# Layer 1's query projection moved ahead of the head loop, and three elementwise steps of the heads moved to GpSimd

## The chip, the core and the metric

The kernel runs on one core of one Trainium2 chip. The metric is device time in microseconds, the median of several executions; a profile is one further execution, recorded by the hardware profiler. PE is TensorE (matmuls and transposes), DVE is VectorE, ACT is ScalarE, POOL is GpSimd, SP is the engine that issues most DMAs.

## The reference

Two layers work on 1024 latent tokens of width 1024 and 256 context tokens. Layer 0 (attention heads beside mLSTM heads) is the same before and after. Layer 1 has 16 bidirectional gated-linear-attention heads with 128 keys and 128 values each; only the latent stream is returned. What it computes:

```python
def project(h):                                    # h: (1, T, 1024), w_in: (1024, 5 * 2048)
    q, f_fwd, f_bwd, i, z = _split_cols(h @ w_in, C_SIZES)       # each 2048 = 16 heads x 128
    def decay(f_pre):
        f = lb + (1.0 - lb) * jax.nn.sigmoid(f_pre)
        return 1.0 - f, jnp.log(f)                 # k and the log decay
    return (silu(q), i, (decay(f_fwd), decay(f_bwd))), z
...
def step(S, xs):                                   # per head, both directions, chunk by chunk
    qc, kc, vc, lfc = xs
    b = jnp.cumsum(lfc, axis=2)
    o = einsum('bhtk,bhkv->bhtv', qc * jnp.exp(b), S)
    pair = jnp.exp(where(tri, b[:, :, :, None, :] - b[:, :, None, :, :], -inf))
    a = einsum('bhtk,bhtsk->bhts', qc, pair * kc[:, :, None, :, :])
    o = o + einsum('bhts,bhsv->bhtv', a, vc)
    bL = b[:, :, -1:, :]
    S = jnp.exp(bL[:, :, 0])[..., None] * S + einsum('bhsk,bhsv->bhkv', kc * jnp.exp(bL - b), vc)
...
return (_rms(o, h_norm) * silu(z)) @ w_out         # added to x with a gate
```

## The kernel before

**Products in two parts.** An fp32 operand is split into a high part (a cast on ACT, line 74) and a low part (the difference, on DVE, line 75, function `split`). A dense product is three matmuls per 128 rows of the contraction: high by high, high by low, low by high (`dense`, lines 127 to 129). In the profile they are the matmuls `mm<-hh,wh`, `mm<-hl,wh`, `mm<-hh,wl`; `hh` and `hl` are the two parts of the normalised input, which stay in SBUF, transposed.

**The stage ahead of the heads** (pool `qv`) computes v and z of layer 1 for all heads, 512 columns at a time. It treats the product as a 2 by 2 product of quarters and forms it with seven products in place of eight (`q_seven`: sums of input quarters `s1` to `s4` made once, sums of weight quarters made per group by `q_form`). For z each of the seven products is two units of 12 matmuls with 512 moving columns (`tr=True`); a unit's result goes to PSUM, is combined on DVE, passed through silu (`z_sink`: sigmoid on ACT, multiplication on DVE) and stored to DRAM by a POOL DMA, as `zd[head]`. The groups run in the order v0 v1 z0 v2 z1 v3 z2 z3 (v0 by the plain eight products).

**The heads.** `build` loops over 16 heads. Three things of neighbouring heads are issued in each turn:

- `hg_intra` of head h: for each half of 512 tokens (first half 1, then half 0) K = 1 - F, two products Q = q x F, then seven levels (`hg_level`). A level copies a selection of K (`gksel`, ACT, line 1226; at level 0 also one of Q, line 1230), multiplies it with Q on PE (line 1235, four 128x128 products), takes the result over into `gA` under a mask (DVE; at level 6 two copies on ACT, lines 1245 and 1246), and multiplies K and Q by decays on DVE (line 1256). After level 0, `hg_diag` uses the sum of the two K directions, made on DVE (line 1243). At the end K is transposed on PE (line 1210) into PSUM tiles of tag `tr` and copied to `gkn`, one direction by ACT, the other by DVE (line 1212). `gK` has two buffers, one for each half, so a half's next K cannot be written before these transposes have read the last one.
- `hg_scan` of head h-1: 15 state products (`s<-gv,gkn`, line 1281) with a DVE step each, and three output products per chunk (`acc`, lines 1297 to 1299); four ACT squares and a POOL reciprocal root per four chunks (lines 1305, 152, 154).
- `hg_parts` of head h+1: the projections f of both directions (512, 512 and 256 tokens each) and q (512 and 512), each with 24 matmuls per token block, and `hg_ctx`. The weights come as 128 columns in two pieces of 256 KB, each split by line 74 and line 75. They wait in a ring of four slabs, that is two blocks of weights.

PSUM has eight banks: tag `mm` two (projections), `tr` two (transposes), `s` three, `acc` one. A tile scheduler orders each engine's instructions by priority and readiness in its own model; on the chip every engine then runs its list strictly in that order.

Of the kernel before, what the change touches and what calls it, by code (L numbers as in the profile page):

```python
# [9 lines left out]
F32 = mybir.dt.float32  # L10
F32R = mybir.dt.float32r
U8 = mybir.dt.uint8
AF = mybir.ActivationFunctionType
# [5 lines left out]
P = 128  # L19
# [27 lines left out]
class Prog:  # L47
# [24 lines left out]
    def split(self, hi, lo, x):  # L72
        nc = self.nc
        nc.scalar.copy(hi, x)  # L74
        nc.vector.tensor_tensor(out=lo, in0=x, in1=hi.bitcast(F32), op=ALU.subtract)  # L75
# [747 lines left out]
    def hg_parts(self, h, pool, w=None):  # L823
# [20 lines left out]
        def q(t0):  # L844
            ps = self.ps("mm", [P, 512])
            self.proj_tr(ps, weights(0), 0, t0, 512)
            t = st["q"][t0 // 512] = self.t(pool, [P, 512], F32, "gq", 2)
            nc.scalar.activation(t, ps, AF.Sigmoid)
            nc.vector.tensor_tensor(out=t, in0=t, in1=ps, op=ALU.mult)
# [158 lines left out]
    def z_sink(self, j, pool):  # L1008
        def sink(c, t, m, o):
            g = self.t(pool, [P, 512], F32, "qg", 2)  # L1010
            self.nc.scalar.activation(g, o, AF.Sigmoid)
            self.nc.vector.tensor_tensor(out=o, in0=g, in1=o, op=ALU.mult)
            s = t // self.half * 512
            self.nc.gpsimd.dma_start(out=self.zd[4 * j + 2 * c + t % self.half // 2, :, s : s + 512], in_=o)

        return sink
# [161 lines left out]
    def hg_intra(self, st, pool, slots):  # L1178
# [8 lines left out]
        for hf in (1, 0):  # L1187
            F, q = st["F"][hf], st["q"][hf]
            K = self.t(pool, [P, 2, n], F32, "gK", 2)
            nc.vector.tensor_scalar(out=K, in0=F, scalar1=-1.0, scalar2=1.0, op0=ALU.mult, op1=ALU.add)  # L1190
            Q = self.t(pool, [P, 2, n], F32, "gQ", 4)
            for d in range(2):
                nc.vector.tensor_tensor(out=Q[:, 1 - d, :], in0=q, in1=F[:, d, :], op=ALU.mult)
            A = self.t(pool, [P, 4, P], F32, "gA", 4)
            hv[hf] = dict(Q=Q, A=A, T=F, K=K)
# [8 lines left out]
        for hf in (1, 0):  # L1204
            H = hv[hf]
            H["kn"] = []
            for d in range(2):
                p = self.ps("tr", [P, 4, P])
                for c in range(4):
                    nc.tensor.transpose(p[:, c, :], H["K"][:, d, c * P : (c + 1) * P], self.ident)  # L1210
                k_ = self.t(pool, [P, 4, P], F32, "gkn", 4)
                (nc.vector.tensor_copy if d else nc.scalar.copy)(k_, p)
                H["kn"].append(k_)
# [3 lines left out]
    def hg_level(self, H, lev, pool):  # L1217
# [21 lines left out]
        if lev == 0:  # L1239
# [3 lines left out]
            nc.vector.tensor_tensor(out=H["ks"], in0=K[:, 0, :], in1=K[:, 1, :], op=ALU.add)  # L1243
# [26 lines left out]
    def hg_scan(self, st, halves, pool):  # L1270
# [60 lines left out]
    def build(self):  # L1331
        self.six = None
        tc, nc, a = self.tc, self.nc, self.a
        dma = nc.sync.dma_start
        with ExitStack() as es:
# [12 lines left out]
            self.zd = self.scratch(dr, "zd", [16, P, LAT])  # L1348
            self.md_all = self.scratch(dr, "md", [20, T, 256])
# [208 lines left out]
            with l1:  # L1558
                with tc.tile_pool(name="qv", bufs=1) as pool, self.pp.phase(sa=4):
                    self.q_open([(0, 2), (2, 2)], a["wc"], (pool, "qo", 3), (pool, "b11", 4), (pool, "sr", 2))  # L1560
                    cs = lambda z, j: [(3 + z) * 2048 + j * 512 + c * 256 for c in range(2)]
                    raw = self.q_raw(pool, cs(0, 0), ("12", "22"))
                    self.q_plain(raw, early, self.v_sink(0), pool)
                    self.q_sums(pool, "2", S)
                    for x in ("v1", "z0", "v2", "z1", "v3", "z2", "z3"):
                        z, j = x[0] == "z", int(x[1])
                        self.q_seven(self.q_raw(pool, cs(z, j)), S, self.z_sink(j, pool) if z else self.v_sink(j), pool, tr=z)
# [11 lines left out]
                scan, done = [], [None, None]  # L1579
                for h in range(16):  # L1580
# [12 lines left out]
                    done, st = [done[1], st], nxt  # L1593
                self.hg_y(14, done[0], pool, self.yd2)
# [178 lines left out]
```

## Time and profile before

| | us |
|---|---|
| time, median of 3 runs (3436.0 to 3436.93) | 3436.47 |
| the profiled execution's own time | 3440.12 |
| its span in the profile | 3438.4 |
| PE busy | 3398.6 (99%) |
| DVE busy | 2347.2 (68%) |
| ACT busy | 1498.9 (44%) |
| POOL busy | 502.9 (15%) |

The stage ahead of the heads lies at about 1850 to 2160 us of the span, the heads at about 2160 to 3290 us. An engine's busy time is the union of its instructions; matmuls are pipelined, so two that follow each other overlap in the record and the distance of their starts says more than their duration. An fp32 product of 128x128 is recorded as two matmuls ("x8" for four products). In a row of the timeline the columns are start, duration, engine, line, operation, result and operands, shapes and count; the bracket gives the idle time before it and what ended that.

### The profile page before, as it was taken

To read this page: it belongs to the slowest core of one execution; us is meant where nothing else is said; L and a number is where in the kernel's file an instruction comes from. 1 tells how busy PE (TensorE), PEld (TensorE's weight loads), DVE (VectorE), ACT (ScalarE), POOL (GpSimd) and SP (SyncE) were. 2 spreads that over 40 slices of the span, in tenths; PEclk is the share of its full clock that TensorE was granted. 3 is DMA by queue.
4 is the path that set the end of the run, shared out by engine and by line. 5 is a ranking of instruction groups with operands and counts; after the bars stand their busy time and mean duration, and the time that the engine had idled before them with its cause. 6 is when DMAs were issued, how large, how long until landed. Compare 5 with 4: busy or idle time off the path is not lost. (4 is left out here: it accounts for less than half of the span.)

```text
span 3438.4 us, 62336 instructions
## 1 busy us (share of the span) xinstructions
PE 3398.6 (99%) x23360; PEld 3060.1 (89%) x23360; DVE 2347.2 (68%) x5814; ACT 1498.9 (44%) x3469; POOL 502.9 (15%) x834
## 2 busy tenths in 40 slices
PE   7999999999999999999999999999999999999999
PEld 5689999999999999988879998899999999999887
DVE  5477747666666654667678666577777777777855
ACT  5322245555544534556546323444444444444431
POOL 3111121222222211212212111000000000000010
PEclk9999999999999999999999999999999999999999
DMA  8543322332223235465483332211111111111345
GB/s 264 190 134 110 120 69 57 88 88 78 80 77 88 77 91 160 139 181 162 141 255 128 109 106 91 77 41 61 54 50 53 60 54 50 53 60 55 114 140 179
DMA packets 359518, 359.63 MB, mean 105 GB/s; under 512 B 30584, under 2 KB 304184, under 8 KB 359088
## 3 DMA queue, kind: packets, MB, share of 16 engines
q1 hardware_dynamic: 315248, 246.36, 24.3%
q0 software_dynamic: 43824, 109.16, 9.2%
q8 instruction: 184, 3.01, 0.4%
q14 instruction: 118, 0.97, 0.1%
q10 hardware_dynamic: 144, 0.13, 0.0%
HBM read 271.98 MB, written 83.42 MB: 103 GB/s over the span
## 5 line engine op out<-in xcount | busy, mean ns | idle before, releaser
L129 PE MATMUL mm<-hh,wl 128*128 128x512 f32 (+1 forms) x1564 | 567.8, 363 | 1.8 <-DVE wl L75 1.8
L127 PE MATMUL mm<-hh,wh 128*128 128x512 f32 (+1 forms) x1564 | 565.0, 361 | 0.1
L128 PE MATMUL mm<-hl,wh 128*128 128x512 f32 (+1 forms) x1564 | 564.6, 361 | 0.0
L127 PE MATMUL mm<-wh,hh 128*128 128x256 f32 x1880 | 541.6, 289 | 2.5 <-ACT wh L74 2.4
L128 PE MATMUL mm<-wl,hh 128*128 128x256 f32 x1880 | 542.1, 289 | 0.1
L129 PE MATMUL mm<-wh,hl 128*128 128x256 f32 x1880 | 541.9, 289 | 0.2 <-DVE hl L75 0.2
L127 PEld LDWEIGHTS mm<-wh,hh 128*128 128x128 f32 x1880 | 358.0, 191 | 5.1 <-ACT wh L74 2.6
L128 PEld LDWEIGHTS mm<-wl,hh 128*128 128x128 f32 x1880 | 358.7, 191 | 3.7 <-issue 1.7
L129 PEld LDWEIGHTS mm<-wh,hl 128*128 128x128 f32 x1880 | 358.4, 191 | 3.4 <-issue 1.6
L127 PEld LDWEIGHTS mm<-hh,wh 128*128 128x128 f32 x1564 | 296.3, 189 | 42.5 <-issue 4.2
L128 PEld LDWEIGHTS mm<-hl,wh 128*128 128x128 f32 x1564 | 296.1, 189 | 41.0 <-issue 4.2
L129 PEld LDWEIGHTS mm<-hh,wl 128*128 128x128 f32 x1564 | 295.8, 189 | 40.8 <-DVE wl L75 2.0
L74 ACT CAST wh<-wraw 128x512 fp32r<-128x512 f32 x292 | 179.8, 621 | 267.3 <-PE mm L128 157.9
L1226 ACT COPY gksel<-gK 128x512 f32<-128x512 f32 x224 | 148.3, 663 | 274.6 <-PE s L1235 262.8
L75 DVE TENSOR_TENSOR wl<-wraw,wh 128x512 fp32r<-128x512 f32 x292 | 197.0, 684 | 58.6 <-ACT wh L74 56.4
L1235 PE MATMUL s<-gQ,gksel 128*128 128x128 f32 x1536 | 202.1, 276 | 0.0
L1235 PEld LDWEIGHTS s<-gQ,gksel 128*128 128x128 f32 x1536 | 192.6, 191 | 5.8
L776 PE MATMUL mm<-woh,yh 128*128 128x512 f32 (+1 forms) x420 | 167.6, 399 | 2.4 <-ACT yh L74 2.4
L778 PE MATMUL mm<-woh,yl 128*128 128x512 f32 (+1 forms) x420 | 167.1, 399 | 0.5 <-DVE yl L75 0.4
L777 PE MATMUL mm<-wol,yh 128*128 128x512 f32 (+1 forms) x420 | 165.1, 394 | 0.0
L1256 DVE TENSOR_TENSOR gQ<-gQ,gT 128x256 f32<-128x256 f32 x384 | 143.1, 413 | 21.2 <-PE s L1235 21.2
L1248 DVE COPY_PREDICATED gA<-glm,s 128x512 f32<-128x512 uint8 x160 | 117.2, 733 | 54.5 <-PE s L1235 54.5
(592 smaller groups left out, 7971.5 us busy)
## 6 DMA issues: line engine op xcount, KB each, us to landing
wraw<-in_wc_dram SPq DMA_DIRECT2D x130, 256.0 KB, 3.0
wraw<-yd SPq DMA_DIRECT2D x116, 256.0 KB, 4.2
wraw<-in_wab_dram SPq DMA_DIRECT2D x98, 256.0 KB, 3.3
md<-ev POOLq DMA_DIRECT2D x78, 256.0 KB, 2.8
adar<-in_wada_dram POOLq DMA_DIRECT2D x16, 1024.0 KB, 5.9
b<-in_wc_dram SPq DMA_DIRECT2D x62, 256.0 KB, 3.1
adar<-in_wada_dram SPq DMA_DIRECT2D x16, 512.0 KB, 11.1
wraw<-in_wab_dram SPq DMA_DIRECT2D x64, 128.0 KB, 2.7
```

Of the source, the lines that this page charges most:

```text
L74: nc.scalar.copy(hi, x)
L75: nc.vector.tensor_tensor(out=lo, in0=x, in1=hi.bitcast(F32), op=ALU.subtract)
L127: mm(ps, lhsT=lh(k), rhs=rh(k), start=(first and k == 0), stop=False)
L128: mm(ps, lhsT=lh(k), rhs=rl(k), start=False, stop=False)
L129: mm(ps, lhsT=ll(k), rhs=rh(k), start=False, stop=(last and k == nk - 1))
L776: mm(ps, lhsT=yh[:, k, :], rhs=w.h(k)[:, cols], start=(k == 0), stop=False)
L777: mm(ps, lhsT=yh[:, k, :], rhs=w.l(k)[:, cols], start=False, stop=False)
L778: mm(ps, lhsT=yl[:, k, :], rhs=w.h(k)[:, cols], start=False, stop=(k == 7))
L1226: nc.scalar.copy(ksel.rearrange("p (b s i) -> p b s i", s=2, i=h), pick(K))
L1235: nc.tensor.matmul(pa[:, c, :].rearrange("p (b s i) -> p b s i", s=2, i=h), lhsT=ksel[:, c * P : (c + 1) * P], rhs=qp[:, c * nbc : (c + 1) ...
L1248: nc.vector.copy_predicated(A, self.lmask[:, lev - 1, :].unsqueeze(1).to_broadcast([P, 4, P]), pa)
L1256: nc.vector.tensor_tensor(out=t[:, i, :, s, :], in0=t[:, i, :, s, :], in1=bc(tot), op=ALU.mult)
```

## The change

q of layer 1 is no longer computed head by head. It becomes four further groups of `q_seven` in the stage ahead, in the order v0 v1 z0 q0 v2 z1 q1 v3 q2 z2 q3 z3, is passed through the same silu, and stored to a new DRAM tensor `qd`; a head loads its two halves of q by two SP DMAs of 256 KB.

Inside the loop over heads (not in the projections of head 0 ahead of it) the low parts of weights are made on POOL; K = 1 - F and the sum of the K directions move from DVE to POOL. All four `gkn` copies of a head are now on ACT. The state product of chunk 7 takes its PSUM tile from tag `tr` in place of `s`.

```diff
     def split(self, hi, lo, x):
         nc.scalar.copy(hi, x)
-        nc.vector.tensor_tensor(out=lo, in0=x, in1=hi.bitcast(F32), op=ALU.subtract)
+        (self.lo or nc.vector).tensor_tensor(out=lo, in0=x, in1=hi.bitcast(F32), op=ALU.subtract)
...
         def q(t0):
-            ps = self.ps("mm", [P, 512])
-            self.proj_tr(ps, weights(0), 0, t0, 512)
             t = st["q"][t0 // 512] = self.t(pool, [P, 512], F32, "gq", 2)
-            nc.scalar.activation(t, ps, AF.Sigmoid)
-            nc.vector.tensor_tensor(out=t, in0=t, in1=ps, op=ALU.mult)
+            nc.sync.dma_start(out=t, in_=self.qd[h, :, t0 : t0 + 512])
...
-            nc.vector.tensor_scalar(out=K, in0=F, scalar1=-1.0, scalar2=1.0, op0=ALU.mult, op1=ALU.add)
+            nc.gpsimd.tensor_scalar(out=K, in0=F, scalar1=-1.0, scalar2=1.0, op0=ALU.mult, op1=ALU.add)
...
-                (nc.vector.tensor_copy if d else nc.scalar.copy)(k_, p)
+                nc.scalar.copy(k_, p)
...
-            nc.vector.tensor_tensor(out=H["ks"], in0=K[:, 0, :], in1=K[:, 1, :], op=ALU.add)
+            nc.gpsimd.tensor_tensor(out=H["ks"], in0=K[:, 0, :], in1=K[:, 1, :], op=ALU.add)
...
-            u = self.ps("s", [P, P])
+            u = self.ps("s" if c < 7 else "tr", [P, P])
...
-                    for x in ("v1", "z0", "v2", "z1", "v3", "z2", "z3"):
+                    for x in ("v1", "z0", "q0", "v2", "z1", "q1", "v3", "q2", "z2", "q3", "z3"):
...
+                self.lo = nc.gpsimd
                 for h in range(16):
```

The change also gives the scheduler another order. Two places matter below, both at the border between two heads.

PE, before: from the last transposes of a head's K (half 0) on. In the names, `tr` is a PSUM tile of transposes, `gK` the head's K, `s<-gv,gkn` a state product of the scan, `gvT` the context values, and `mm` with a 128x512 shape a projection for the next head.

```order
L1210 MATMUL tr_31281<-ident_75,gK_30594 128x128 x4
L1281 MATMUL s_31301<-gv_31017,gkn_31272 128x128
L1152 MATMUL tr_31408<-ident_75,gvT_31406 128x128 x2
L129 MATMUL mm_31473<-hh_22231,wl_31474 128x512
L127 MATMUL mm_31473<-hh_22231,wh_31475 128x512
L1281 MATMUL s_31305<-gv_31017,gkn_31272 128x128
L128 MATMUL mm_31473<-hl_22232,wh_31475 128x512
```

Twenty-four 128x512 projections and several small products stand between these transposes and the next head's first level product (`s<-gksel,gksel`, line 1235), at every border from the second to the fourteenth. PE, after, at every second border (six of them), from the products of level 6 (`s<-gQ,gksel`, line 1232) on:

```order
L1232 MATMUL s_32006<-gQ_31421,gksel_32004 128x128 x2
L1296 MATMUL acc_31872<-gS_6349_31974,gQ_30141 128x128
L1232 MATMUL s_32006<-gQ_31421,gksel_32004 128x128 x2
L1207 MATMUL tr_32035<-ident_76,gK_31419 128x128 x4
L1207 MATMUL tr_32042<-ident_76,gK_31419 128x128 x4
L1278 MATMUL s_32066<-gv_31842,gkn_32033 128x128
L1278 MATMUL s_32070<-gv_31842,gkn_32033 128x128
L1232 MATMUL s_32078<-gksel_32076,gksel_32074 128x128 x4
L1278 MATMUL tr_32062<-gv_31842,gkn_32033 128x128
L1149 MATMUL tr_32169<-ident_76,gvT_32167 128x128 x2
L1232 MATMUL s_32096<-gksel_32094,gksel_32092 128x128 x4
L1162 MATMUL tr_32180<-ident_76,gEc_32174 128x128 x4
```

Both halves' first level products now stand there without a projection between them and the transposes; at the other borders 13 projections of 512 columns and 23 of 256 remain between.

ACT, before, at the same border: copies of transposed K (`gkn`), selections of the new K and Q (`gksel`), level 6 results (`gA`), squares (`gon`), then the projection's evacuation (`gF<-mm`).

```order
L1212 COPY gkn_33382<-tr_33377 128x512
L1226 COPY gksel_33416<-gK_33392 128x512
L1245 COPY gA_32696<-s_33307 64x4x64
L1246 COPY gA_32696<-s_33307 64x4x64
L1230 COPY gksel_33418<-gQ_33394 128x512
L1305 ACTIVATE gon_32690,gss_33257<-acc_33150 128x128 x4
L1245 COPY gA_32702<-s_33322 64x4x64
L1246 COPY gA_32702<-s_33322 64x4x64
L1154 COPY gvc_33514<-tr_33511 128x256
L840 ACTIVATE gF_33575<-mm_33576 128x512
```

ACT, after, at the border of the PE rows above, in the change's own line numbers:

```order
L1223 COPY gksel_32074<-gK_32050 128x512
L1242 COPY gA_31418<-s_31991 64x4x64
L1243 COPY gA_31418<-s_31991 64x4x64
L1227 COPY gksel_32076<-gQ_32052 128x512
L1302 ACTIVATE gon_31412,gss_31979<-acc_31872 128x128 x4
L1242 COPY gA_31424<-s_32006 64x4x64
L1243 COPY gA_31424<-s_32006 64x4x64
L1209 COPY gkn_32040<-tr_32035 128x512
L1209 COPY gkn_32047<-tr_32042 128x512
L1223 COPY gksel_32092<-gK_32056 128x512
L1227 COPY gksel_32094<-gQ_32058 128x512
L840 ACTIVATE gF_32233<-mm_32234 128x512
```

The two copies that DVE made have joined the row, and the next head's second selection and the evacuation of a projection stand behind them.

More of the change, by code (lines that the diff above doesn't have):

```diff
@@ L1013, in sink @@
             s = t // self.half * 512
[L1014 removed]
+            self.nc.gpsimd.dma_start(out=dst[4 * j + 2 * c + t % self.half // 2, :, s : s + 512], in_=o)
         return sink
@@ L1331, in build @@
     def build(self):
-        self.six = None
+        self.six = self.lo = None
         tc, nc, a = self.tc, self.nc, self.a
```

13 lines of the change are left out of this document (8 added, 5 removed).

## The prediction

> **What bounds the kernel now.** I read the page first, then the busy times by stage, then one head's period: its waits and its timeline on each engine.
>
> ```profile
> PE 3398.6 (99%) x23360; PEld 3060.1 (89%) x23360; DVE 2347.2 (68%) x5814; ACT 1498.9 (44%) x3469; POOL 502.9 (15%) x834
> 2160.00:3213.00 1053.00, 1053.00 (x6935) 955.58 (x6934) 788.58 (x1935) 448.03 (x939) 55.53 (x80) 1.00 0.18 55
> 1850.00:2160.00 310.00, 310.00 (x1955) 280.60 (x1954) 214.26 (x336) 104.40 (x180) 43.37 (x72) 1.00 0.31 108
> 2377.39:2446.18 68.79, 68.79 (x460) 62.58 (x459) 52.40 (x130) 29.24 (x64) 4.15 (x7) 1.00 0.18 55
> ```
>
> After the stretch and its length, a row of the second kind gives the busy time of PE, PE's weight loads, DVE, ACT and POOL, then granted clock, DMA share and GB/s. Two stages matter: the heads (2160 to 3213) and the stage ahead of them (1850 to 2160). In both PE is busy all the time, at full clock. The last row is one period of the head loop, from one head's first reciprocal root to the next's. DVE works for 52.40 of its 68.79 us, ACT for 29.24, POOL for 4.15. The waits in this period bear it out: the longest are those of ACT and DVE for PE's products, and no row of that view has PE waiting.
>
> ```profile
> ACT gksel L1226 <- PE s L1235: 17.6, 10, 4.9
> DVE gA L1248 <- PE s L1235: 2.9, 3, 1.4
> ```
>
> So whatever takes work from PE in either stage shortens the kernel by as much, as long as PE's ordered list finds its operands ready. The whole question is whether it still does.
>
> **The change part by part.**
>
> *The products.* The heads lose 16 x 2 x 24 = 768 matmuls of 512 columns. The stage ahead gains 4 groups x 7 products x 2 units x 12 = 672 of the same shape: 96 fewer. The price of one is the distance of starts:
>
> ```profile
> 2395.00 0.40 PE L127 MATMUL mm<-hh,wh 128*128 128x512 f32 x1
> 2398.42 0.40 PE L127 MATMUL mm<-hh,wh 128*128 128x512 f32 x1
> 2100.00:2150.00 50.00, 50.00 (x219) 40.76 (x218) 37.40 (x59) 19.02 (x32) 5.96 (x11) 1.00 0.21 77
> ```
>
> The first two rows, in the heads, are 15 matmuls apart: 3.42 / 15 = 0.228 us. The third is a stretch inside groups z2 and z3: 50 / 219 = 0.228 us. Hence 175 us go, 153 come, and PE's work falls by 96 x 0.228 = **21.9 us**. The new groups run at PE's pace like the z groups: DVE works there for 37.40 of 50 us and ACT for 19.02, with everything that a group needs (weight sums, low parts, silu) in it.
>
> *The transfers.* Each is priced by its counterpart: storing q by the stores of z, loading q by the loads of z.
>
> ```profile
> zd<-qo POOLq DMA_DIRECT2D x16, 256.0 KB, 2.5
> gz<-zd SPq DMA_DIRECT2D x32, 256.0 KB, 2.7
> ```
>
> 32 stores join POOL's queue in the stage ahead, 32 more loads of weights SP's. In the heads 32 loads of q take the place of 32 weight pieces of the same 256 KB, so SP's queue has as many entries as before. q is issued six and seven slots of a turn ahead, some 40 us before it is needed, and DMA is busy for 0.18 of the period. I cost this at nothing; without that cover it would be 2.7 us per load.
>
> *DVE and ACT in the heads.* The rows of what leaves DVE, from 12 periods:
>
> ```profile
> L75 DVE TENSOR_TENSOR wl<-wraw,wh 128x512 fp32r<-128x512 f32 x98 | 65.7, 680 | 0.0
> L849 DVE TENSOR_TENSOR gq<-gq,mm 128x512 f32<-128x512 f32 x26 | 17.7, 682 | 13.8 <-ACT gq L848 13.8
> L1243 DVE TENSOR_TENSOR gksel<-gK 128x512 f32<-128x512 f32 x24 | 16.4, 681 | 0.0
> L1212 DVE COPY gkn<-tr 128x512 f32<-128x512 f32 x24 | 16.3, 680 | 0.0
> L1190 DVE TENSOR_SCALAR gK<-gF 128x1024 f32<-128x1024 f32 x24 | 16.3, 679 | 0.0
> ```
>
> Per head 8 + 2 + 2 + 2 + 2 = 16 instructions of 0.68 us leave: 10.9 us, so 41.5 remain. The period without q's 48 matmuls is 68.8 - 10.9 = 57.9 us, so DVE's share falls a little, from 76 to 72%. None of this is on the path by itself. ACT loses two casts and two sigmoids and gains two copies, about 0.6 us each: 28 of 58 us.
>
> *POOL.* It gains eight two-operand instructions of 512 columns and two one-operand ones of 1024 per head. No row shows such lengths. The nearest:
>
> ```profile
> L152 POOL TENSOR_SCALAR ar<-ar 128x8 f32<-128x8 f32 x40 | 9.1, 228 | 213.2 <-DVE ar L590 144.0 <-DVE anm L678 68.7
> L152 POOL TENSOR_SCALAR mr<-mss 128x1 f32<-128x1 f32 x40 | 8.8, 220 | 76.4 <-ACT mlo L559 76.0
> masks.py:197 POOL MEMSET ident<- 128x128 f32 x1 | 0.2, 205 | 0.3 <-POOLq L1761 0.3
> L1761 POOL MEMSET const-float32-1.0<- 128x1 f32 x1 | 0.1, 100 | 0.0
> ```
>
> A fill costs (205 - 100) / 127 = 0.8 ns per column, arithmetic on one operand (228 - 220) / 7 = 1.1. From below, 512 columns take 0.5 us and 1024 0.9; from above, with two operands read in turn, 0.22 + 512 x 2.3 ns = 1.4 us, and 0.22 + 1024 x 1.1 ns = 1.4 us for K. I take the arithmetic rows, 1.4 us: 14 us more per head, POOL at 18 of 58 us. [...]
>
> Who waits for POOL? The low parts: weights wait in a ring of two blocks, and between the end of one block and the first use of the one that replaces it lie the 24 short matmuls of `hg_ctx` and two levels' products, about 5 us, against a cast and 1.4 us. The sum of K is used by `hg_diag`, behind both first level products. K itself is used by the first selection of the next head, and there the border between two heads is to be looked at.
>
> *The border.* Before, 24 projections of 512 columns (5.5 us) lie on PE between the last transposes and the first level product, which covers all that ACT does there. After the change six borders have none: the second half's level product follows closely, and the banks for a further projection are not free, since their evacuation stands behind on ACT. Let me time ACT's list from where PE has finished level 6 of half 1:
>
> ```profile
> 2389.54 0.59 ACT L1212 COPY gkn<-tr 128x512 f32<-128x512 f32 x1 [0.59 <-PE tr L1210]
> 2390.03 0.85 ACT L1226 COPY gksel<-gK 128x512 f32<-128x512 f32 x1
> 2392.15 0.85 ACT L1230 COPY gksel<-gQ 128x512 f32<-128x512 f32 x1
> 2393.02 0.28 ACT L1305 ACTIVATE gon<-acc 128x128 f32<-128x128 f32 x1
> 2394.03 0.36 ACT L1245 COPY gA<-s 64x256 f32<-64x256 f32 x1
> 2394.80 0.37 ACT L1154 COPY gvc<-tr 128x256 f32<-128x256 f32 x1
> 2401.78 0.86 ACT L1226 COPY gksel<-gK 128x512 f32<-128x512 f32 x1 [0.83 <-PE s L1235]
> 2402.55 0.85 ACT L1230 COPY gksel<-gQ 128x512 f32<-128x512 f32 x1
> 2392.96 0.60 PE L1210 MATMUL tr<-ident,gK 128*128 128x128 f32 x4
> 2393.40 0.39 PE L1281 MATMUL s<-gv,gkn 128*128 128x128 f32 x2
> 2406.51 1.05 PE L1235 MATMUL s<-gksel,gksel 128*128 128x128 f32 x8
> 2407.40 1.06 PE L1267 MATMUL s<-gq,gksel 128*128 128x128 f32 x8
> ```
>
> By the distances of these starts: two `gA` copies 0.77, selection of Q 0.87, four squares 1.01, two `gA` 0.77, two `gkn` 0.98, selection of K 0.77, of Q 0.87: 6.0 us until half 0 can be multiplied. PE has in the same time, up to that product, 12 products of 0.89 / 4 = 0.22 us and 10 transposes of 0.11 us: 3.8 us. So PE stands still for 2.2 us, and for 2.5 with the hand-overs (about 0.1 us each; my choice): 6 x 2.5 = **15 us**. K is not what ends it: POOL's K takes 1.4 us while ACT waits for level 6 anyway. At the other borders 13 long and 23 short projections (5.5 us) cover it.
>
> *The sum.* 3440.1 (the profiled execution) - 21.9 + 15 = 3433.2. That execution lies 3.65 us above the median, 3436.47; against the median the same -7 us make **3429.6**. A measurement of this kernel can tell about 0.2% (7 us) from no change.
>
> **The rivals.**
>
> *The whole saving arrives.* If the six stops don't cost PE anything (the level 6 products may already be late, or ACT early), 3436.5 - 21.9 = 3414.6. For it speaks that no PE wait is seen before; against it that ACT's list above is longer than PE's by rows of this trace.
>
> *Every border stops.* If the covered borders lose 1.5 us each too (9 x 1.5 = 13.5 us), 3429.6 + 13.5 = 3443. The five microseconds of cover speak against it.
>
> *POOL and DVE exclude each other, and the kernel gets slower.* At 3222.67 a reciprocal root on POOL took twice its usual time while DVE was dense:
>
> ```profile
> 3222.67 2.09 POOL L154 TENSOR_TENSOR gss<-gss,mhalf 128x4 f32<-128x4 f32 x1
> 3275.19 1.03 POOL L154 TENSOR_TENSOR gss<-gss,mhalf 128x4 f32<-128x4 f32 x1
> L1193 DVE TENSOR_TENSOR gQ<-gq,gF x64: 678/682/693, 2188.9 to 3220.3; 128x512 f32<-128x512 f32 x64
> ```
>
> So the two do meet. In this trace POOL gives way: DVE's products of two SBUF operands (the third row: minimum, median, maximum) never stretch. But POOL reads four columns here and would read 512. If DVE stands still while POOL reads, 10 instructions of 1.4 us per head fill DVE to 41.5 + 14 = 55.5 of 58 us, and four of them (K, sum, K, sum) fall on the border, where DVE makes the new Q and the first updates of K. If half of these 5.6 us reaches PE at each of 15 borders, 42 us: 3429.6 + 42 = 3472. It decides from 0.5 us per border on (7 / 15). [...] The trace agrees that POOL waits (2.09 against 1.03 us); that DVE does, no row shows. [...]
>
> **How the numbers follow.** The forecast's own case 40%; its spread (stops of 1.7 to 3.3 us, 3425 to 3435) lies on both sides of the 0.2% mark, 22 of the 40 faster. The whole saving 20%, faster. Every border stops 12%: 7 no change, 5 slower. Exclusion 28%: 25 slower, 3 so mild that nothing changes. Faster 42%, no change 28%, slower 30%. The range reaches from the whole saving (3414) up into the exclusion, 3466, which leaves out its dearer third and little below.
>
> **What would show it.** In the profile after, the stage ahead should be 153 us longer with PE busy throughout, a pair of head periods should take 2 x 57.9 + 2.5 us, and the waits should have PE rows for the first time: level 0's product and the state product in `tr` waiting for ACT. POOL's instructions should have 1 to 1.5 us. I am wrong if DVE's rows of two operands rise above 0.68 (0.42 for 256 columns), if PE waits on POOL's low parts or on K, or if no PE wait appears at all.

## The result, and the profile after

The changed kernel takes 3457.91 us (median of 4 runs, 3455.63 to 3461.67) against 3436.7 us before on the same chip: ratio 1.0062 [1.005, 1.0075], some 21 us slower. The forecast was 3429.6. The profiled execution took 3458.57 us, its span 3456.7.

The page's busy line, after, and then the busy times by stage: a stretch in the stage ahead, two periods of the head loop, and the eight periods behind them.

```profile
PE 3390.1 (98%) x23264; PEld 3048.5 (88%) x23264; DVE 2410.6 (70%) x5738; ACT 1539.0 (45%) x3533; POOL 738.4 (21%) x1022
```

```profile
2200.00:2250.00 50.00, 50.00 (x219) 40.77 (x218) 35.02 (x56) 17.53 (x29) 4.87 (x9) 1.00 0.35 116
2432.85:2552.93 120.08, 116.82 (x822) 107.67 (x821) 97.90 (x227) 56.55 (x123) 36.31 (x32) 1.00 0.20 62
2552.93:3035.34 482.41, 468.84 (x3282) 432.23 (x3281) 392.30 (x905) 226.39 (x489) 144.06 (x129) 1.00 0.20 62
```

The stage ahead runs as dense as it did: 219 matmuls in 50 us, PE never out of work. The heads do not. A pair takes 120.08 us with PE busy for 116.82; over eight heads 13.6 us are empty, where before PE was busy throughout. PE has 96 matmuls fewer and is busy for 8.5 us less, but the span is 18.3 us longer.

The first level product of head 0 closes the stage ahead. Timeline of PE, before and then after:

```profile
2194.20 1.05 PE L1235 MATMUL s<-gksel,gksel 128*128 128x128 f32 x8
```

```profile
2331.83 1.05 PE L1232 MATMUL s<-gksel,gksel 128*128 128x128 f32 x8
```

It comes 137.6 us later. Counted by products it should be 153.2 - 10.9 (head 0's own q) = 142.3 later, so nothing is lost up to here, and 4.7 us are gained. The waits of PE behind it, after (engine, tile and line, what it waited for; total us, times, longest):

```profile
PE s L1232 <- ACT gF L840: 11.2, 6, 1.9
PE mm L776 <- ACT yh L74: 6.9, 4, 3.9
PE s L1232 <- ACT gA L1243: 6.4, 6, 1.1
PE acc L1296 <- DVE gS L1280: 2.3, 6, 0.5
PE tr L1320 <- DVE gon L1304: 0.7, 1, 0.7
```

Six borders stop PE twice each, 1.07 + 1.86 us, 17.6 us together; a short stop at an output product inside the head comes six times; and 7.6 us are lost at the end. Before, the same view held 2.0 us in all (1.1, 0.6 and 0.3).

A wait row leaves out what a late start costs behind it. So I also took every distance between the starts of two matmuls of the heads and the end, and summed what each exceeds its dense distance by, where that is over 0.1 us: 3.7 us before; after, 47.1 us (36.3 in the heads, 1.2 in the first, 9.6 at the end). PE's work fell by 21.9 and its losses rose by 43.4: +21.5 us against +18.3 of the span. The part ahead, 4.7 us shorter than counted, more than pays for the difference. The sum is good to a few us only, since it depends on the dense distances: with the medians of the kernel before (0.230 us for 512 columns, 0.120 for 256, 0.112 for 128) it comes to 3.4 before and 43.0 after, so +17.7 in all.

One border, timeline after (start, duration, engine and line, operation, result and operands, shapes, count, and in brackets the idle time before it):

```profile
2510.15 2.40 DVE L1190 TENSOR_TENSOR gQ<-gq,gF 128x512 f32<-128x512 f32 x2
...
2510.73 1.27 POOL L1240 TENSOR_TENSOR gksel<-gK 128x512 f32<-128x512 f32 x1 [2.54 <-PE s L1232]
...
2511.97 1.49 POOL L1187 TENSOR_SCALAR gK<-gF 128x1024 f32<-128x1024 f32 x1
...
2512.47 1.01 DVE L1255 TENSOR_TENSOR gT<-gT 128x16 f32<-128x16 f32 x1
2512.52 0.37 ACT L1243 COPY gA<-s 64x256 f32<-64x256 f32 x1
2512.91 1.07 ACT L1209 COPY gkn<-tr 128x512 f32<-128x512 f32 x2
...
2512.94 1.16 PE L1232 MATMUL s<-gksel,gksel 128*128 128x128 f32 x8 [1.07 <-ACT gA L1243]
...
2514.97 0.84 ACT L1227 COPY gksel<-gQ 128x512 f32<-128x512 f32 x1
2515.57 0.68 DVE L1238 TENSOR_TENSOR gA<-s,glm 128x512 f32<-128x512 f32 x1
2515.72 0.58 ACT L840 ACTIVATE gF<-mm 128x512 f32<-128x512 f32 x1
2516.40 1.13 PE L1232 MATMUL s<-gksel,gksel 128*128 128x128 f32 x8 [1.86 <-ACT gF L840]
```

The first product waits for ACT's copies of level 6, as forecast. The second should start when ACT's selection of Q is done, at 2515.81. It starts at 2516.40, 0.6 us later. The view puts this down to ACT's `gF`, which this product does not read. What it needs is a bank of tag `s`. Two of the three hold early state products (`s<-gv,gkn`), the third the first product's own result, which DVE empties only with L1238, ending at 2516.25; `late_states` below tests this reading. And DVE is late: two Q products took 2.40 us in place of 1.36 while POOL added up K (L1240), and a product of 16 columns took 1.01 while POOL made the next K (L1187).

The prices, from the groups by line, after, before, and after again for POOL (busy us, mean ns; then idle time):

```profile
L1253 DVE TENSOR_TENSOR gK<-gK,gT 128x256 f32<-128x256 f32 x320 | 148.7, 508 | 1.8 <-ACT gksel L1223 1.3
...
L1190 DVE TENSOR_TENSOR gQ<-gq,gF 128x512 f32<-128x512 f32 x51 | 39.6, 813 | 0.1
...
L1255 DVE TENSOR_TENSOR gT<-gT 128x16 f32<-128x16 f32 x26 | 16.7, 642 | 0.1
```

```profile
L1256 DVE TENSOR_TENSOR gK<-gK,gT 128x256 f32<-128x256 f32 x262 | 98.4, 416 | 0.0
...
L1193 DVE TENSOR_TENSOR gQ<-gq,gF 128x512 f32<-128x512 f32 x44 | 29.1, 683 | 0.0
...
L1258 DVE TENSOR_TENSOR gT<-gT 128x16 f32<-128x16 f32 x20 | 3.4, 168 | 0.3
```

```profile
L75 POOL TENSOR_TENSOR wl<-wraw,wh 128x512 fp32r<-128x512 f32 x81 | 113.2, 1402 | 350.3 <-ACT wh L74 347.5 <-ACT gknc L1164 2.7
L1240 POOL TENSOR_TENSOR gksel<-gK 128x512 f32<-128x512 f32 x26 | 37.2, 1431 | 59.7 <-PE s L1232 59.7
L1187 POOL TENSOR_SCALAR gK<-gF 128x1024 f32<-128x1024 f32 x26 | 34.3, 1319 | 109.2 <-PE tr L1207 105.2 <-ACT wh L74 2.4 <-DVE gA L1245 1.6
```

POOL costs what was estimated (1.4 us). DVE's products of two SBUF operands stretch by 92, 130 and, for 16 columns, 474 ns on average: DVE is held up, as the rival on POOL and DVE has it.

### The profile page after: what moved, and what is told of

Read it like the earlier page. It is cut to its first block, busy times and chain, and to the rows that moved or that the text cites. A ratio compares the mean times of both kernels' runs of the same rounds, so it can differ in the third digit from the quotient of the medians.

```text
span 3456.7 us, 62612 instructions
## 1 busy us (share of the span) xinstructions
PE 3390.1 (98%) x23264; PEld 3048.5 (88%) x23264; DVE 2410.6 (70%) x5738; ACT 1539.0 (45%) x3533; POOL 738.4 (21%) x1022
## 4 chain that ended last, share of the span: by engine, by line
PE 91%; DVE 3%; DMA 2%; ACT 2%; issue 1%; SPq 0%; POOL 0%; ACTq 0%; DVEq 0%; POOLq 0%
PE mm L127 14%; PE mm L129 14%; PE mm L128 14%; PE s L1232 5%; PE mm L776 3%; PE mm L778 3%; PE mm L777 3%; PE sa L127 3%; PE sa L129 3%; PE sa L128 3%; PE acc L728 3%; PE tr L708 2%; PE acc L511 2%; PE s L518 2%; PE tr L127 2%; PE tr L129 1%
## 5 line engine op out<-in xcount | busy, mean ns | idle before, releaser
L127 PE MATMUL mm<-hh,wh 128*128 128x512 f32 (+1 forms) x1324 | 474.8, 359 | 0.4
L128 PE MATMUL mm<-hl,wh 128*128 128x512 f32 (+1 forms) x1324 | 472.3, 357 | 0.0
L129 PE MATMUL mm<-hh,wl 128*128 128x512 f32 (+1 forms) x1324 | 470.1, 356 | 1.8 <-DVE wl L75 1.8
L127 PEld LDWEIGHTS mm<-hh,wh 128*128 128x128 f32 x1324 | 251.6, 190 | 36.0 <-issue 4.2
L128 PEld LDWEIGHTS mm<-hl,wh 128*128 128x128 f32 x1324 | 251.9, 190 | 32.0 <-issue 4.2
L129 PEld LDWEIGHTS mm<-hh,wl 128*128 128x128 f32 x1324 | 251.2, 190 | 32.5 <-DVE wl L75 2.0
L74 ACT CAST wh<-wraw 128x512 fp32r<-128x512 f32 x260 | 159.6, 620 | 193.2 <-PE mm L128 82.2
L74 ACT CAST wh<-b 128x512 fp32r<-128x512 f32 x178 | 110.3, 620 | 235.0 <-PE sa L129 58.1
L75 POOL TENSOR_TENSOR wl<-wraw,wh 128x512 fp32r<-128x512 f32 x92 | 128.5, 1402 | 371.9 <-ACT wh L74 358.5
L1253 DVE TENSOR_TENSOR gK<-gK,gT 128x256 f32<-128x256 f32 x384 | 174.8, 498 | 2.8 <-ACT gksel L1223 2.0
```

The source lines that it names most:

```text
L75: (self.lo or nc.vector).tensor_tensor(out=lo, in0=x, in1=hi.bitcast(F32), op=ALU.subtract)
L127: mm(ps, lhsT=lh(k), rhs=rh(k), start=(first and k == 0), stop=False)
L128: mm(ps, lhsT=lh(k), rhs=rl(k), start=False, stop=False)
L129: mm(ps, lhsT=ll(k), rhs=rh(k), start=False, stop=(last and k == nk - 1))
L1253: nc.vector.tensor_tensor(out=t[:, i, :, s, :], in0=t[:, i, :, s, :], in1=bc(tot), op=ALU.mult)
```

## The experiments

Two theories stood at the start. A: what counts is PE's cover at the border, that is, products that keep PE busy while the other engines make its next operands; take q out and the stops come, wherever the small steps run. B: POOL's reads hold DVE up, and that is the price. Edits are against the changed kernel unless said otherwise.

**The parts apart.** `q_alone` moves q and leaves the rest as before; `pool_alone` leaves q in the heads and moves the three steps to POOL.

```diff
 q_alone
-                self.lo = nc.gpsimd
-            nc.gpsimd.tensor_scalar(out=K, in0=F, ...)
+            nc.vector.tensor_scalar(out=K, in0=F, ...)
-            nc.gpsimd.tensor_tensor(out=H["ks"], ...)
+            nc.vector.tensor_tensor(out=H["ks"], ...)
-                nc.scalar.copy(k_, p)
+                (nc.vector.tensor_copy if d else nc.scalar.copy)(k_, p)
-            u = self.ps("s" if c < 7 else "tr", [P, P])
+            u = self.ps("s", [P, P])
 pool_alone (against before)
-        nc.vector.tensor_tensor(out=lo, ...)
+        (self.lo or nc.vector).tensor_tensor(out=lo, ...)      # nc.gpsimd in the heads; K and ks too
```

> The projection of q is moved as in the change; the low parts, 1 - F, the sum of K and the copies of transposed K stay where they were before, and so does the PSUM tag of the state product. Theory A (PE loses its cover at the border of two heads, and that is what the change pays for): in this order no border has a projection between the last transposes of K and the first level product, thirteen times, so PE stops at about 2 us each at thirteen borders, and runs out of work at the end as after the change (9 us): 3436.5 - 21.9 + 26 + 9 = 3450, with no stretched instruction on DVE. Theory B (POOL and DVE exclude each other, and that is what the change pays for): without POOL's work the saving arrives, 3415 to 3425.

> The kernel before, with q still projected in the heads, and only three things moved to POOL: low parts of the heads' weights, 1 - F, the sum of K. Theory A (cover): every border keeps nineteen or more projections of 512 columns, so PE never waits for DVE, although DVE's instructions with two SBUF operands should stretch to about 0.8 us for 512 columns as after the change: 3437, within 5 us. Theory B (exclusion): the stretched list of DVE reaches PE at every head, 15 times 1.5 us or more: 3455 to 3475.

Measured: `q_alone` 3470.84 us, 1.0103 [1.0086, 1.012]; `pool_alone` 3438.45 us, 1.0006 [0.9996, 1.0015]. The main waits of PE in `q_alone`, then DVE's groups in `pool_alone`:

```profile
PE tr L1162 <- ACT gvc L1151: 11.3, 13, 0.9
PE tr L1320 <- ACT gknc L1164: 8.9, 13, 0.7
```

```profile
L1256 DVE TENSOR_TENSOR gK<-gK,gT 128x256 f32<-128x256 f32 x264 | 126.2, 516 | 6.9 <-ACT gksel L1226 6.0
...
L1193 DVE TENSOR_TENSOR gQ<-gq,gF 128x512 f32<-128x512 f32 x44 | 36.2, 864 | 0.9 <-PE acc L1299 0.2
```

The busy times of eight heads of the same kernel:

```profile
2441.84:2992.31 550.47, 550.47 (x3666) 500.71 (x3665) 433.59 (x937) 234.79 (x505) 161.90 (x145) 1.00 0.18 54
```

The stretch is as large as after (516 and 864 against 508 and 813 ns), and it costs nothing: PE is busy for all of the 550.47 us. So the stretch alone is no loss where q's products cover it. Moving q alone loses without it: over eight heads `q_alone` has 32 DVE instructions fewer than before (1001 against 1033), 21.8 us at 0.68 us each, and DVE works 23.4 us less (395.73 against 419.14). Theory A had the place right, thirteen borders and ACT, but its 3450 was 21 us too low. PE stops ahead of the transposes of the context and of the outputs, not ahead of the first level product; the waits are 1.55 us a border, but by start distances, with the medians above as dense ones, the heads lose some 47 us. The other parts of the change repay some 13 of the 35 us; with them seven of the thirteen bare borders have projections again.

**What POOL costs after the change.** A fill on POOL writes and reads nothing. `low_fills` fills the low parts with zeros on POOL in place of subtracting; `low_k_fills` also fills K with 0.5. The instructions of PE, ACT and DVE stay, with one output product a place earlier in `low_k_fills`; the low parts, and then K, are left out of the result.

```diff
 low_fills
-        (self.lo or nc.vector).tensor_tensor(out=lo, in0=x, in1=hi..., op=ALU.subtract)
+        nc.gpsimd.memset(lo.bitcast(F32), 0.0) if self.lo else nc.vector.tensor_tensor(out=lo, ...)
 low_k_fills, in addition
-            nc.gpsimd.tensor_scalar(out=K, in0=F, scalar1=-1.0, ...)
+            nc.gpsimd.memset(K, 0.5)
```

> The changed kernel with every instruction in the same order on PE, ACT and DVE; only the low parts of the heads' weights are left out: POOL fills them with zeros in place of the subtraction, so POOL reads nothing from SBUF in eight of its ten instructions per head. K and its sum stay on POOL. Theory A (cover, with DVE's stretching as a part of the stops): the stop inside the head where PE waits for a state from DVE (1.1 us, six times) goes, and the border keeps most of its 3.65 us, since K and its sum are what is late or stretches there: 3458 - 7 = 3451. Theory B (exclusion pays for most): 3458 - 20 = 3438 or less, and DVE's products of 256 columns go back to 0.42 us.

> The changed kernel with low parts of the heads' weights and 1 - F left out: POOL fills both with constants, so only the sum of K reads SBUF on POOL. The order on PE, ACT and DVE is that of the changed kernel but for one product of a head's output that stands one place earlier. If POOL's reading of F behind DVE's list at the border is what makes the first level's result late (the second stop there, 2.1 us six times), that stop shrinks to the 1.3 us at which ACT has its selections ready: 3451 - 5 = 3446. If ACT's list alone sets both stops, nothing changes: 3451.

Measured: 3451.31 us, 1.0046 [1.0031, 1.0061], and 3444.96 us, 1.0023 [1.0014, 1.0033]. DVE's K products in `low_fills`, then the waits of PE in `low_k_fills` and DVE and POOL at one of its borders:

```profile
L1253 DVE TENSOR_TENSOR gK<-gK,gT 128x256 f32<-128x256 f32 x325 | 125.5, 429 | 1.5 <-ACT gksel L1223 1.0
```

```profile
PE s L1232 <- ACT gksel L1227: 7.9, 6, 1.3
PE mm L776 <- ACT yh L74: 7.0, 4, 3.5
PE s L1232 <- ACT gA L1243: 6.4, 6, 1.1
```

```profile
2506.90 2.39 DVE L1190 TENSOR_TENSOR gQ<-gq,gF 128x512 f32<-128x512 f32 x2
2507.48 1.27 POOL L1240 TENSOR_TENSOR gksel<-gK 128x512 f32<-128x512 f32 x1 [2.72 <-PE s L1232]
...
2508.68 0.95 POOL L1187 MEMSET gK<- 128x1024 f32 x1
...
2509.22 0.16 DVE L1255 TENSOR_TENSOR gT<-gT 128x16 f32<-128x16 f32 x1
```

Without the reads of the low parts DVE is back at 429 ns, the stop at the output products is gone from the view and 6.6 us return. Without K's reads too, the second stop of a border falls from 1.86 to 1.32 us and is now set by ACT's selection of Q, and 6.35 us more return. The six shorter stops are 3.2 of these; in the profiled executions `low_fills` also had a lower mean clock, 0.994 against 0.996, and the same 3282 matmuls of eight heads kept PE busy for 467.23 us there and for 464.59 in `low_k_fills`. The split into 6.6 and 6.35 is rough, since each interval is 3 to 5 us wide on either side. So B accounts for some 13 us of the 21. A fill is also shorter on POOL (527 in place of 1402 ns, K 951 in place of 1319), but it is the reading that counts: beside K's fill the product of 16 columns takes 0.16 us, while beside the sum of K, which still reads, the Q products still take 2.39. What remains at a border, (7.9 + 6.4) / 6 = 2.4 us, is ACT's list alone, and it is what the forecast had (2.2 to 2.5).

**Covering the border.** If cover is all that is missing, products put at the bare place should win the saving back. `hold_ctx` holds the 24 short context products on PE until the last transposes of K; `spread` in addition holds a long projection until both first level products, with the `gkn` copies split over ACT and DVE as before; `spread_more` also moves the context's part of one f there.

```diff
 hold_ctx
+        self.after_kt(self.mms[0])       # first context product, ordered behind the last transpose of K
 spread, in addition
+            if d == 0 and t0 == 512 and 0 in self.last_lv:
+                self.after(self.mms[0], self.last_lv[0])
-                nc.scalar.copy(k_, p)
+                (nc.vector.tensor_copy if d else nc.scalar.copy)(k_, p)
```

> The changed kernel with all its moves; the 24 context projections of 256 columns of a head (the first of the value path) are held back until the last transposes of K of the head before, so that PE has 2.7 us of products there and the projections of the following head stand between the first level products, at every border. Theory A (cover): the six stops of 3.65 us go, and some of the waits for the state with them: 3458 - 22 = 3436, down to 3430. Theory B (exclusion): the order does not matter, DVE is late anyway, 3450 to 3460.

> The changed kernel with two of the four copies of transposed K back on DVE, and with two ties on PE's order: the 24 context products of a head come behind the last transposes of K of the head before (as in the run that held them), and the first projection for the following head comes behind both first level products. So every border has 21 products of 256 columns (2.4 us) ahead of the first level product and no projection of 512 columns, and all 96 of those are left to the seven levels. Theory E (where the projections stand decides: the run that held the context products was slow because up to 36 products of 512 columns moved into the border with them and left the levels bare): the stops shrink to about 0.5 us per head, and with the saving and the 9 us at the end 3436 - 22 + 8 + 9 = 3431. Rival (DVE is late for the levels whenever the border is covered, wherever the projections stand): 3455 to 3500.

> As the run above, but the second direction's projection of the context (24 products of 256 columns) is put behind the transposes too: 5.4 us of products at every border ahead of the first level product, 2.7 us fewer in the levels. Theory E: the border needs less than this, so the levels lose 2.7 us that they could use: slower than the run above by up to 15 x 2.7 = 40 us, 3435 to 3470. Rival: as above, both the same.

Measured: 3503.63 us, 1.0194 [1.0179, 1.021]; 3529.95 us, 1.0267 [1.0252, 1.0283]; 3496.92 us, 1.0169 [1.0154, 1.0184]. All three are worse than the change as it stood, and `hold_ctx` and `spread` lie above every forecast made for them. A falls as a recipe: the stops reappear elsewhere, as if PE had enough work for one place only. `spread_more`, with still more products at the border, is 33 us faster than `spread`; the theory behind it had it slower. The waits of PE in `hold_ctx`:

```profile
PE s L1239 <- DVE gA L1252: 37.6, 14, 3.6
PE acc L1303 <- DVE gS L1287: 8.8, 5, 1.8
```

and in `spread`:

```profile
PE acc L1304 <- DVE gon L1314: 49.8, 12, 4.5
```

I read the first as a level's product standing before banks of `s` that DVE has not emptied. The second is the first output product of a chunk group standing before the single `acc` bank, and all that is behind it on PE's list stands too. Is it the bank?

**The banks.** `spread_acc` orders that output product behind both first level products. `spread_banks` also moves all `gkn` copies to ACT and orders a state product behind them, so that it does not hold a bank of `s` early. `late_states` does this last alone, on the changed kernel.

```diff
 late_states (and in spread_banks)
+            if d and c == 6:
+                self.after(x, self.last_lv[0])
-        return [do(back, 7, 6, 5), do(back, 4, 3), do(back, 2, 1)] + ...
+        return [do(back, 7), do(back, 6, 5, 4), do(back, 3, 2, 1)] + ...
```

> The run with the spread projections, with one more tie: the first output product of a head's scan (it writes the one bank of tag acc) comes behind the first level products of the following head, where in that run it stood ahead of the second one and PE waited 4.5 us per head for DVE to empty the bank. If the failure of that run was this one wait, and the projections stand well otherwise (theory E), it falls by 13 x 4.8 us and by the half clock that follows long stops: 3530 - 62 - 10 = 3458 or less, down to 3431. If it only moves (the head's chain through DVE sets the pace), PE waits elsewhere and the time stays above 3490.

> The spread order once more (all copies of transposed K on ACT as in the change, context products at every border, first projections behind the first level products, first output product behind them too), and the state products of chunk 6 and later ones come behind both first level products, so that no state product holds a bank of tag s while these two are multiplied. Bank theory (the second first-level product waits for the bank that DVE empties of the first, because early state products hold the other two of three): the wait of 3.7 us at each border goes, 3515 - 14 x 4 - 10 of half clock = 3450 or less, down to 3431 where nothing takes its place. Rival (DVE's list at the border is the pace, the wait only gets another name: transposes of gEc, states): 3490 or more.

> The changed kernel with one tie alone: the state products of chunk 6 and later come behind both first level products. In this order thirteen borders have no projection, as six have after the change, but the banks of tag s are free. Bank theory: the second stop there (2.1 us, for DVE to empty the first result) shrinks to the 1.3 us at which ACT has the selections, so a border costs 2.9 us, and there are thirteen: 3458 - 22 + 38 = 3474. Rival (DVE's list): 13 x 3.65, 3484 or more.

Measured: 3515.08 us, 1.0226 [1.021, 1.0242]; 3504.7 us, 1.0191 [1.0176, 1.0206]; 3480.8 us, 1.0123 [1.0106, 1.0139]. The waits of PE in `spread_acc` and then in `late_states`:

```profile
PE s L1242 <- DVE gA L1248: 51.2, 15, 5.1
```

```profile
PE tr L1282 <- ACT gkn L1213: 14.8, 12, 1.2
PE s L1236 <- ACT gksel L1231: 12.8, 12, 1.1
```

In `late_states` the reading of the second stop is borne out: with the banks free, the first level product stops 1.07 us for ACT's selection, and for no bank. But the held state product now stops for its own operand, `gkn`, and because the border is thereby ordered the same way in every head, it stops at twelve borders and not six. The time lies between the two forecasts, 3474 and 3484, so it is the view that decides. In `spread_acc` 49.8 us at `acc` became 51.2 at `gA`. Six orders, and in the views shown each time the same sort of loss under another name.

**Is it DVE or the chain?** `thin` leaves out the high-by-low product in heads 1 to 15, a third of the projections; `thin_fills` is `thin` with the two fills.

```diff
 thin
-            mm(ps, lhsT=lh(k), rhs=rl(k), start=False, stop=False)
+            self.lo or mm(ps, lhsT=lh(k), rhs=rl(k), start=False, stop=False)
```

> The changed kernel, with the products of high by low parts left out of the heads' projections (a third of them, 10.0 us of PE's work per head; heads 1 to 15 only). Theory C: the time per head stays at 57 to 60 us, since the chain of seven levels through ACT, PE and DVE and the border set it: 3410 to 3455, with PE's waits growing by what was taken away. Theory D (PE's work still sets the heads, and only the borders cost): 15 x 10 us go, 3310 to 3320.

> The changed kernel without the products of high by low parts in the projections of heads 1 to 15 (as in the run that left them out), and with POOL's low parts and 1 - F replaced by fills, so that DVE's list is not stretched by them. In the run without fills a head took 54.6 us, DVE worked for 50.3 of it and PE for 50.2, PE's starts alone would give 47.8. Theory F (DVE's list, with its stretched instructions, is the next bound of a head): DVE falls to 45 us and the head to 50, 3372 - 15 x 4.6 = 3303. Rival (the chain of hand-overs between the engines at the border and in each level is the bound, whatever DVE's list is): a head stays above 53 us, 3350 to 3370.

Measured: 3372.01 us, 0.981 [0.9796, 0.9825], and 3363.2 us, 0.9784 [0.9768, 0.98]. Eight heads by busy time, `thin` and then `thin_fills`:

```profile
2535.51:2972.53 437.02, 401.60 (x2832) 372.70 (x2832) 402.58 (x905) 222.74 (x489) 144.20 (x128) 0.97 0.22 68
```

```profile
2529.08:2956.46 427.38, 393.38 (x2836) 365.46 (x2835) 353.21 (x905) 223.91 (x489) 95.98 (x128) 0.99 0.23 70
```

Some 10 us of projections per head leave PE (32 products of 0.228 us and 24 of 0.12), but the period falls from 60.3 to 54.6 us: 5.7. Both theories missed: C had 57 to 60 us per head, D the full 10 us back. No engine is full now, PE and DVE at 92% each. The fills take 6.2 us per head off DVE and bring 1.2, as the rival had it (above 53 us). So it is not DVE's work. What is left is the chain of hand-overs between PE, ACT and DVE within a head, which with this order would take some 53 to 55 us; that is an inference, the chain itself was not followed.

**Half of it.** `half_q` takes q by DMA in the even heads alone, so that each pair keeps one head's 48 products as cover. Three variants try to mend its end: `half_q_kn` splits the `gkn` copies again, `half_late` does so in heads 14 and 15 alone and takes tag `s` there, `half_late_s` takes tag `s` in head 15's scan alone.

```diff
 half_q
+            if h % 2 == 0:
                 nc.sync.dma_start(out=t, in_=self.qd[h, :, t0 : t0 + 512])
+                return
+            ps = self.ps("mm", [P, 512])      # else the projection of before
...
-                    for x in ("v1", "z0", "q0", "v2", "z1", "q1", "v3", "q2", "z2", "q3", "z3"):
+                    for x in ("v1", "z0", "q0", "v2", "z1", "v3", "q1", "z2", "z3"):
```

> The changed kernel, but only the heads with an even number get q from the stage ahead (two groups of seven products in place of four, made of the columns of heads 0, 2, 4, 6 and 8, 10, 12, 14); the odd heads project q in the heads, as before the change. All other moves stay. Theory C (what a head can do at best is set by its own chain through DVE and ACT, about 60 us; PE's products beyond the head's own only fill that time, and with 57.8 us of them PE stops): a pair of heads has 2 x 57.8 + 10.9 = 126.6 us of PE work for 2 x 60 us of chain, so the border stops go and half of the saving stays: 3436 - 11 + 3 = 3428. Theory B (each move to POOL or each border costs by itself): half of the loss remains, 3447.

> The kernel in which only heads with an even number get q from the stage ahead, with two of the four copies of transposed K back on DVE. The wait for ACT's copy at the last border (1.0 us) goes and perhaps with it one stretch of half clock (1.7 us): 3435 - 2 = 3433. If PE sets the heads throughout, nothing else can change.

> The kernel in which only even heads get q from the stage ahead; for heads 14 and 15 alone two copies of transposed K are on DVE and the state product of chunk 7 is in tag s, as before the change, so that in this order products of the output projection stand between the last transposes and the first level product of head 15. If what is left of the loss there is the end's stops (1.0 + 2.3 us of waits at the last border, 1.7 us of half clock behind them, 1.6 us at the output projection), 3 to 6 us of them go: 3429 to 3432. If the end is bound by the last head's own chain, the same as without this: 3435.

> As the run above, but only the PSUM tag of the state product is undone, and only for head 15, whose scan comes last: the transposes that waited 2.3 us for the bank of that product no longer share it. 2 to 4 us less than without it, 3431 to 3433; or the same, if the wait for ACT's copies of K takes its place.

Measured: 3434.93 us, 0.9995 [0.9985, 1.0004]; 3437.63 us, 0.9997 [0.9988, 1.0007]; 3434.82 us, 0.9991 [0.9982, 1.0]; 3435.09 us, 0.9992 [0.9984, 1.0001]. Eight heads of `half_q`, and its waits of PE in the heads and the end:

```profile
2494.47:3002.59 508.12, 507.91 (x3474) 465.76 (x3473) 402.76 (x912) 235.86 (x505) 156.46 (x137) 1.00 0.20 59
```

```profile
PE tr L1172 <- DVE gS L1290: 2.3, 1, 2.3
PE mm L776 <- ACT yh L74: 1.6, 1, 1.6
PE tr L1159 <- ACT gkn L1219: 1.0, 1, 1.0
```

With POOL's reads in place as after, PE is full again in the heads: 63.5 us per head, and half the saving (-11 us) is there. The time, 3435, lies between the two theories (3428 and 3447) all the same. By start distances it loses 12.0 us, 3.6 in the heads and 8.4 at the last border and the end, against 3.7 in all before; -11 + 8.3 is the -3 measured. The three variants move the stops at the end, not the time; where 2 to 6 us were hoped for, none came. Two to three microseconds are no more than a measurement here can tell from nothing, so no version run clearly beats the kernel before.

## Why the prediction was wrong

**What bounds the kernel.** Right: PE's list, and the question was whether it still finds its operands ready. It does not.

**The products, -21.9 us.** Right: the stage ahead stays at 0.228 us per product and head 0's first level product comes 137.6 us later, against 142.3 counted.

**The transfers, nothing.** Right as far as seen: no wait of PE leads to a load of q.

**The six stops, 15 us.** The place, the number and the price of ACT's list were right: 2.4 us per border in `low_k_fills`, against 2.2 to 2.5. The term was still too small. By waits the border costs 2.94 us, and with the first products that start late behind it 3.65 by start distances, 22 us in all. The first step that failed is that ACT's list was taken to be the only one: with q's projections gone, the next thing in line is a bank of `s`, emptied by a DVE that POOL holds up. This is 7 us of the 25 between the forecast change (-7) and that of the span (+18.3); most of the rest is the last term below.

**"K is not what ends it".** Wrong in effect. K's own 1.4 us are covered, but POOL's reads hold DVE up at the border: the sum of K holds the Q products (2.40 us for two in place of 1.36), K the decay product of 16 columns (1.01 in place of 0.17). With the reads of the low parts gone, taking K's away was enough to bring the second stop back to ACT's list, and 6.35 us returned.

**The low parts.** PE never waits for them, as forecast; their cost came through DVE, to an output product that waits for a state (`acc <- gS`). Taking their reads away returned 6.6 us.

**Exclusion as a rival.** The stretch is there, its size was not: DVE works 392.30 / 8 = 49.0 us per head, not 41.5 as forecast nor 55.5 as in the rival, and 13 us of the price of 42 arrive. It comes with POOL's reads: DVE's K products took 508 ns on average with the low parts read, 429 with them filled, 416 before. What failed is the form: I gave the forecast a DVE without any stretch and put the stretch beside it, as a case. The two belong in one sum. `pool_alone` (3438.45 us) shows that the stretch costs nothing while there is cover, and `q_alone` (3470.84) that the cover goes with q, so the change brought both halves of one loss together. The range held the measured time only because it reached up into this rival.

**The covered borders and the rest of the head, nothing.** Inside the heads the six state stops cost about 1.1 us each by start distances. The three stretches at half clock (below) cost 5.1 us by estimate, and the end some 9 us. All three were costed at nothing, and this is the larger step that failed: together some 19 us (the end's stretch counted once), against a gain of 4.7 that was not forecast either, in the part ahead. `low_k_fills` still loses 9.4 us at the end, so POOL is not the cause there; the last head's result goes through DRAM while PE is out of other products. What in the change opened this gap stays open.

That PE's saved products arrive as saved time is therefore refuted for this order. Whether some order keeps the whole saving is open: six others kept less.

## What to carry to other kernels

Work that an engine does without waiting may still be somebody's cover: before taking it away, time the chain of hand-overs that it hides, all of it, banks included. A sum over the period is not enough: the changed kernel's 57.9 us of products per head exceed the 53 to 55 us that a head took in the `thin` runs, and PE still stopped where the border was bare. A slowdown that cost nothing under cover (K products of 516 ns in `pool_alone`) came due when the cover went (508 ns after), so put such slowdowns into the sum, not into a rival. And try a smaller dose before another order: half of the move left PE full in the heads (though the time was no better than before), six new orders of the whole did not.

## What the runs showed of the hardware

Between the first border and the last matmul of the changed kernel PE was granted half its clock three times, twice of these behind short gaps. Busy times behind the border at 2757 and at the end of the kernel, after (behind the five busy times stand the granted clock, DMA share and GB/s):

```profile
2757.80:2761.00 3.20, 3.20 (x19) 3.20 (x18) 3.04 (x11) 1.24 (x2) 1.32 (x1) 0.55 0.02 5
3364.00:3368.00 4.00, 0.30 (x2) 0.00 (x0) 1.39 (x2) 0.51 (x1) 0.00 (x0) 1.00 0.99 323
3370.00:3372.00 2.00, 2.00 (x6) 1.52 (x6) 1.59 (x3) 1.43 (x3) 0.00 (x0) 0.50 1.10 362
```

Short products of 256 columns start 0.21 us apart in the first stretch, in place of 0.12. Such a stretch lasted 3.41 us each of the three times (at 2758, 3120 and 3369) and costs, as an estimate, half of that, 1.7 us. The gap at the end was 3.9 us long, but at the borders no gap was: 1.07 and 1.86 us within five microseconds went before it. Of six alike borders two were followed by it, so the gaps alone do not decide it. In `hold_ctx` and `spread`, with more stops, the mean clock over eight heads was 0.97 and 0.96, against 1.00 after. What does decide it, no run shows.

Short DVE products of two SBUF operands were held up beside POOL's reads as long ones were. At the border shown above the product of 16 columns started while POOL made K and ended with it (2513.48 and 2513.46). After the change it went from 168 to 642 ns on average; with 32 and 64 columns, which have another place in the order, it took 188 and 215, against 181 and 212. In `pool_alone` these two took 266 and 370, and 8 columns 556 in place of 161.
